# A hybrid decoder trunk: how the running-sum rows reach the SSD scan, and where its squares lie

## The chip, the cores and the metric

The kernel runs on one core of a Trainium2 chip. The metric is the device time of one execution in microseconds (us); the median of three runs counts. The kernel computes in float32.

## What is computed

Two layers and a final norm. The even layer projects the normed input once, and feeds a Mamba-2 SSD branch and a branch of differential attention; the odd layer is a gated linear recurrence. The change touches the SSD branch alone. Its scan, for 16 heads of 64 in 4 groups, sequence length 1024, chunks of 128:

```python
def ssd_scan(x, dt, A, Bm, Cm):
    ...
    a_cs = jnp.cumsum(a, axis=-1)
    CB = jnp.einsum("bclgn,bcsgn->bcgls", Cc, Bc)
    scores = CB[:, :, :, None] * jnp.exp(segsum(a))
    y_diag = jnp.einsum("bcgrls,bcsgrp->bclgrp", scores, X)
    decay_states = jnp.exp(a_cs[..., -1:] - a_cs)
    states = jnp.einsum("bclgn,bcgrl,bclgrp->bcgrpn", Bc, decay_states, X)
    ...
    y_off = jnp.einsum("bclgn,bcgrpn,bcgrl->bclgrp", Cc, prev, jnp.exp(a_cs))
    return (y_diag + y_off).reshape(b, L, H, P)
...
y = ssd_scan(xs, dt, A, Bm, Cm) + xs * D_skip[:, None]
y_a = rmsnorm(y * jax.nn.silu(z), ssd_norm_w)
```

So the running sum `a_cs` of a head enters twice: as exp of its differences inside a chunk (the scores), and as exp(a_cs) along the rows of the output (`y_off`). The norm at the end needs the sum of the squares of all the gated outputs.

## The kernel before

**Projections.** Activations lie with channels on partitions and time along the row, 1024 long. Each float32 operand is split into a high and a low part, and a product is three matmuls. A piece of a projection is 128 channels by 512 time steps: 24 matmuls of 128x512 (`mm_cm`, L174) into one of two PSUM buffers `pj`. Weights come by SyncE's queue into `w_raw` (L126); ScalarE casts the high part (L132) and VectorE makes the low one (L133). A conv piece is emptied from `pj` by ScalarE (L426, L427); after the fourth, VectorE does the other taps of the convolution (L435), ScalarE a tanh (L438), VectorE a product (L439). A gate piece is emptied by `silu2`: ScalarE's tanh from `pj` into the tile `th` (L232) and VectorE's product of `th` and `pj` into an `A` tile (L233). `pj` is free after L233.

**The scan.** The 32 chunk steps are 4 groups (of 4 heads) by 8 chunks. `weave` lets the steps of group g run between the pieces of the projection of group g+1 (12 pieces: 4 conv pieces of x, 4 of B and C, 4 of the gate z); the steps of the last group run between pieces of the attention's first head (q and k, v, gate). A step has two halves, `first(c)` and, two pieces later, `second(c)`.

- `first(c)` loads the running sum of the group's four heads for this chunk, the same for all 128 partitions (`R`, 128x4x128, L464), into one of three tiles that are used in turn: two called `G`, one `wT`. TensorE transposes x and B and multiplies B by C (L466 to L470) into PSUM tile `s1`; VectorE makes X (L475), GpSimd X times the decay (L478), ScalarE copies B (L479), VectorE masks CB (L480). VectorE subtracts the running sum of the partition's own time step from `R` (L482, four heads), ScalarE takes exp (L484), VectorE multiplies by CB (L485). X, the decayed X, the state and CB lie in one chunk tile `pk` (slots `p0`, `p0` and `bt` in turn).
- `second(c)` is the matmuls with the state, of the new state and of the scores (L502, L505, L508) into PSUM tile `big`; VectorE updates the state (L514, L515). For every second chunk it loads the running sum again for two chunks in another layout, two heads by 64 partitions each (L523, tile `ey`), and takes exp (L525). VectorE multiplies the state's part by it (L529) and adds the other part (L530). After an odd chunk it adds the D skip (L537, from the x tiles in `A`), multiplies by the gate (L540), ScalarE squares the result into a `th` tile (L542), GpSimd adds the squares up (L544, L547), and the result is stored (L548).

**Tiles.** A name in the trace is a slot: `t(tag)` waits until the tile that had the slot last has been read. There is one `th`, one `ey`, one `cm`, one `wT`, one `bt`, two `G`, two `p0`, two `o`, eleven `A`. `cm` is used by the first attention head afterwards, for its bias (loaded by L590, read by L607).

**Order.** In the scan TensorE's order is written out by hand (`manual_schedule`). The order of the other engines and of SyncE's queue is set by the framework's scheduler from the program's dependences.

Of the kernel before, what the change touches and what calls it, by code (L numbers as in the profile page):

```python
# [14 lines left out]
AF = mybir.ActivationFunctionType  # L15
# [4 lines left out]
P = 128  # L20
# [50 lines left out]
def run(pieces):  # L71
    for _ in pieces:
        pass
# [12 lines left out]
def bc(ap, shape):  # L86
    return ap.broadcast_to(shape)


class Net:  # L90
# [115 lines left out]
    def proj_v(self, u):  # L206
        vs = []
        run(self.v_pieces(u, vs))
        return self.v_of(vs)


    def gate_pieces(self, u, tags, gs):
# [240 lines left out]
def ssd_steps(S, g, tiles, ya, at, lag):  # L453


    nc = S.nc
    hs = slice(4 * g, 4 * g + 4)
    X_, sts, eas = {}, {}, {}

    def first(c):  # L460
        x0, x1, Bt, Ct = tiles[:4]
        cs = slice(c * P, c * P + P)
        R = S.t(("G", "G", "wT")[(8 * g + c) % 3], [P, 4, P])
        nc.sync.dma_start(R, bc(S.acs_d[hs, cs].unsqueeze(0), [P, 4, P]))  # L464
        pt = S.ps("s1")
        nc.tensor.matmul(pt[:, 384:512], lhsT=Bt[:, cs], rhs=Ct[:, cs], start=True, stop=True)  # L466
        for b in range(2):
            nc.tensor.transpose(out=pt[:, b * P:b * P + P], in_=(x0, x1)[b][:, cs], identity=S.ident)
        if c < NT - 1:
            nc.tensor.transpose(out=pt[:, 256:384], in_=Bt[:, cs], identity=S.ident)  # L470
        pk = S.t("bt" if (8 * g + c) % 3 == 2 else "p0", [P, 1024])
        X = pk[:, 0:256].rearrange("p (h d) -> p h d", d=64)
        Xd = pk[:, 256:512].rearrange("p (h d) -> p h d", d=64)
        cb, Bk = pk[:, 768:896], pk[:, 896:1024]
        nc.vector.tensor_tensor(X, pt[:, 0:256].rearrange("p (h d) -> p h d", d=64),  # L475
                                bc(S.dt[:, c, hs].unsqueeze(2), [P, 4, 64]), op=ALU.mult)
        if c < NT - 1:
            nc.gpsimd.tensor_tensor(Xd, X, bc(S.dec[:, c, hs].unsqueeze(2), [P, 4, 64]), op=ALU.mult)  # L478
            nc.scalar.copy(Bk, pt[:, 256:384])  # L479
        nc.vector.tensor_tensor(cb, pt[:, 384:512], S.triu, op=ALU.mult)  # L480
        for h in range(4):
            nc.vector.tensor_scalar(R[:, h], R[:, h], S.acs[:, c, 4 * g + h:4 * g + h + 1], 0.0,  # L482
                                    op0=ALU.subtract, op1=ALU.min)
        nc.scalar.activation(R, R, AF.Exp)  # L484
        nc.vector.tensor_tensor(R, R, bc(cb.unsqueeze(1), [P, 4, P]), op=ALU.mult)  # L485
        X_[c] = pk, R

    def second(c):
        Ct = tiles[3]
        cs = slice(c * P, c * P + P)  # L490
        pk, sc = X_[c]
        X = pk[:, 0:256].rearrange("p (h d) -> p h d", d=64)
        Xd = pk[:, 256:512].rearrange("p (h d) -> p h d", d=64)
        sn = pk[:, 512:768].rearrange("p (h d) -> p h d", d=64)
        Bk = pk[:, 896:1024]
        big = S.ps("big")
        pod = big[:, 0:512].rearrange("p (i b t) -> p i b t", i=2, b=2)
        pu = big[:, 512:768].rearrange("p (h d) -> p h d", d=64)
        st = sts.get(c - 1)
        if c > 0:  # L500
            for b in range(2):
                nc.tensor.matmul(pod[:, 0, b], lhsT=st[:, 2 * b:2 * b + 2, :], rhs=Ct[:, cs],  # L502
                                 start=True, stop=True)
        if c < NT - 1:
            nc.tensor.matmul(pu, lhsT=Bk, rhs=Xd, start=True, stop=True)  # L505
        for b in range(2):
            for hh in range(2):
                nc.tensor.matmul(pod[64 * hh:64 * hh + 64, 1, b], lhsT=X[:, 2 * b + hh],  # L508
                                 rhs=sc[:, 2 * b + hh], start=True, stop=True)
        if c < NT - 1:  # L510
            if c == 0:
                nc.scalar.copy(sn, pu)
            else:
                nc.vector.tensor_tensor(sn, st, bc(S.tot[:, c, hs].unsqueeze(2), [P, 4, 64]), op=ALU.mult)  # L514
                nc.vector.tensor_tensor(sn, sn, pu, op=ALU.add)  # L515
            sts[c] = sn
        xs, zg = tiles[:2], tiles[4]
        if c % 2 == 0:

            c2 = slice(c * P, (c + 2) * P)  # L520
            ea = S.t("ey", [P, 2, 256])
            for hh in range(2):
                nc.sync.dma_start(ea[64 * hh:64 * hh + 64],  # L523
                                  bc(S.acs_d[4 * g + hh:4 * g + 4:2, c2].unsqueeze(0), [64, 2, 256]))
            nc.scalar.activation(ea, ea, AF.Exp)  # L525
            eas[c // 2] = ea, S.t("o", [P, 2, 256])
        ea, tt = (z[:, :, (c % 2) * P:(c % 2) * P + P] for z in eas[c // 2])
        if c:
            nc.vector.tensor_tensor(tt, pod[:, 0], ea, op=ALU.mult)  # L529
            nc.vector.tensor_tensor(tt, tt, pod[:, 1], op=ALU.add)  # L530
        else:
            nc.vector.tensor_copy(tt, pod[:, 1])
        if c % 2 == 1:
            t = eas[c // 2][1]
            c2 = slice((c - 1) * P, (c + 1) * P)
            for b in range(2):
                nc.vector.scalar_tensor_tensor(t[:, b], xs[b][:, c2], S.dcol[:, 2 * g + b:2 * g + b + 1],  # L537
                                               t[:, b], op0=ALU.mult, op1=ALU.add)
            for b in range(2):
                nc.vector.tensor_tensor(t[:, b], t[:, b], zg[b][:, c2], op=ALU.mult)  # L540
            sq = S.t("th", [P, 2, 256])
            nc.scalar.activation(sq, t, AF.Square)  # L542
            if g == 0:
                nc.gpsimd.tensor_tensor(S.ysq[:, c2], sq[:, 0], sq[:, 1], op=ALU.add)  # L544
            else:
                for b in range(2):
                    nc.gpsimd.tensor_tensor(S.ysq[:, c2], S.ysq[:, c2], sq[:, b], op=ALU.add)  # L547
            S.ya_stored = nc.sync.dma_start(ya[2 * g:2 * g + 2, :, c2].rearrange("b p t -> p b t"), t)  # L548

    return [(at(c), 2 * c, lambda c=c: first(c)) for c in range(NT)] + [  # L550
        (at(c) + lag, 2 * c + 1, lambda c=c: second(c)) for c in range(NT)]


# [330 lines left out]
def layer0(S, x, x1_d, u1):  # L884
    nc, a = S.nc, S.a
# [4 lines left out]
    run(ssd_pieces(S, u, 0, tiles))  # L890
    with S.tc.issue_after(S.late):
        setup_rest(S)
    S.ysq = S.t("V", [P, L])
    with S.tc.manual_schedule(engines={mybir.EngineType.PE}):
        rest = []
# [266 lines left out]
@with_exitstack  # L1162
def trunk_kernel(ctx, tc, a, out):
    S = Net(ctx, tc, a)
    w0, w1 = wspecs(a)
    S.wspecs = w0 + w1
    x1_d = S.dram.tile([L, D], F32, name="x1_d")
    u1 = [None, None]
    layer0(S, a["x"][0], x1_d, u1)
    layer1(S, x1_d, u1, out)  # L1170
# [24 lines left out]
```

## Time and profile before

| | |
|---|---|
| median of 3 runs | 2238.65 us (2238.03 to 2240.89) |
| the profiled execution | 2242.69 us |
| its span | 2240.9 us |
| PE (TensorE, matmul) busy | 2178.8 us, 97% of the span |
| DVE (VectorE) | 1269.9 us, 57% |
| ACT (ScalarE) | 832.2 us, 37% |
| POOL (GpSimd) | 188.8 us, 8% |

Times in a row of the profile are in us unless marked ns. PE is TensorE's matmuls, PEld its weight loads, SP (or SPq) SyncE and its queue. A row of a timeline has the start, the length, the engine, the line, the operation, the tile written and those read with their shape, a count of instructions that stand together, and in brackets the engine's idle time before it and what ended it. PEclk is the clock that TensorE was granted, as a share of full speed.

### The profile page before, as it was taken

Reading aid. Unit: us, or ns where it says so; the run is one execution under the profiler, and the core shown is the slowest. Engines: PE = TensorE matmul, PEld = TensorE weight load, DVE = VectorE, ACT = ScalarE, POOL = GpSimd, SP = SyncE. Lnnn points to the kernel's source line nnn. Section 1 sums busy time; section 2 is a strip of 40 time slices with the busy share of each in tenths; the row PEclk is TensorE's granted clock in tenths of the full one; section 3 lists DMA queues with packets and bytes.
Section 4 is the critical chain, followed back from the end, with each engine's and each line's share of the span. In section 5 each row is a group of like instructions: output and inputs, shape, how many; then the busy total and the mean of one; then the engine's idle time right before and its main releaser. Section 6 shows DMA issues by size and latency. Waiting matters only on the chain.

```text
span 2240.9 us, 40897 instructions
## 1 busy us (share of the span) xinstructions
PE 2178.8 (97%) x16868; PEld 1920.3 (86%) x16868; DVE 1269.9 (57%) x2864; ACT 832.2 (37%) x1903; POOL 188.8 (8%) x216
## 2 busy tenths in 40 slices
PE   6998998899999999999999999999999999999998
PEld 5787776789898988999988989898989898989998
DVE  4765766565656556755453555555555555557444
ACT  4333333234444545644442323232323222324233
POOL 1001111110000000000010010101010101010000
PEclk9999999999999999999999999999999999999999
DMA  4322233332212221525331111111111111125333
GB/s 138 67 84 66 80 85 81 74 81 64 69 36 67 64 69 41 170 66 159 119 104 39 48 48 48 48 48 48 48 48 48 48 49 48 48 67 165 111 103 122
DMA packets 182256, 169.14 MB, mean 75 GB/s; under 512 B 10239, under 2 KB 163233, under 8 KB 182068
## 3 DMA queue, kind: packets, MB, share of 16 engines
q1 hardware_dynamic: 174564, 152.42, 23.1%
q0 software_dynamic: 3280, 9.90, 2.1%
q10 hardware_dynamic: 4224, 4.19, 0.6%
q8 instruction: 132, 2.16, 0.4%
q14 instruction: 56, 0.46, 0.1%
HBM read 132.66 MB, written 25.43 MB: 71 GB/s over the span
## 4 chain that ended last, share of the span: by engine, by line
PE 51%; DMA 1%; ACT 0%; DVE 0%; issue 0%; POOL 0%; POOLq 0%; ACTq 0%
PE pj L174 24%; PE pj L184 14%; PE big L184 5%; PE big L1051 2%; PE big L1139 1%; PE big L1141 1%; PE s L1128 1%; PE big L1093 1%; PE s L1155 1%; PE s L1122 1%; PE big L1087 0%; PE s L159 0%; DMA ey<-yb 0%; DMA th<-in_lvmask 0%; ACT w_hi L132 0%; DVE w_lo L133 0%
## 5 line engine op out<-in xcount | busy, mean ns | idle before, releaser
L174 PE MATMUL pj<-u,w_hi 128*128 128x512 f32 x3072 | 990.0, 400 | 31.3 <-DVE A L233 21.2
L174 PEld LDWEIGHTS pj<-u,w_hi 128*128 128x128 f32 x3072 | 573.4, 190 | 154.7 <-DVE A L233 23.0
L174 PE MATMUL pj<-u,w_lo 128*128 128x512 f32 x1536 | 607.9, 396 | 0.0
L184 PE MATMUL pj<-w_hi,u 128*128 128x256 f32 x2592 | 492.6, 286 | 1.0 <-DVE A L233 1.0
L184 PEld LDWEIGHTS pj<-w_hi,u 128*128 128x128 f32 x2592 | 409.9, 191 | 3.6 <-DVE A L233 1.4
L184 PE MATMUL pj<-w_lo,u 128*128 128x256 f32 x1296 | 368.3, 284 | 0.0
L174 PEld LDWEIGHTS pj<-u,w_lo 128*128 128x128 f32 x1536 | 291.8, 190 | 61.1 <-issue 0.2
L133 DVE TENSOR_TENSOR w_lo<-w_raw,w_hi 128x1024 fp32r<-128x1024 f32 x168 | 206.3, 1251 | 116.9 <-ACT w_hi L132 116.6
L184 PEld LDWEIGHTS pj<-w_lo,u 128*128 128x128 f32 x1296 | 247.8, 191 | 1.0
L132 ACT CAST w_hi<-w_raw 128x1024 fp32r<-128x1024 f32 x168 | 168.1, 1047 | 188.8 <-PE pj L174 107.6
L233 DVE SCALAR_TENSOR_TENSOR A<-th,pj 128x512 f32<-128x512 f32 x80 | 55.1, 689 | 140.9 <-ACT th L232 140.4
L232 ACT ACTIVATE th<-pj 128x512 f32<-128x512 f32 x96 | 57.2, 596 | 208.5 <-PE pj L174 190.8
L617 ACT ACTIVATE p<-p,mx 128x256 f32<-128x256 f32 (+7 forms) x128 | 98.5, 771 | 72.4 <-DVE mx L613 66.4
L148 POOL TENSOR_TENSOR ro<-rs_t,mhalf 128x4 f32<-128x4 f32 x48 | 52.8, 1100 | 682.4 <-DVE rs_t L147 489.1
L603 PE MATMUL big<-A 128*128 128x512 f32 (+3 forms) x384 | 90.3, 352 | 2.6 <-DMA A<-A 1.3
L968 POOL TENSOR_SCALAR A<-th,fN,fB 128x512 f32<-128x512 f32 x32 | 47.6, 1488 | 470.0 <-ACT th L965 470.0
L637 ACT COPY wT<-s 128x512 f32<-128x512 f32 (+2 forms) x96 | 45.8, 477 | 95.8 <-PE s L635 95.1
L639 PE MATMUL s<-V,wT 128*128 128x128 f32 x576 | 79.7, 275 | 0.6 <-ACT wT L637 0.6
L1035 DVE TENSOR_TENSOR A<-A,p 128x512 f32<-128x512 f32 x96 | 65.8, 686 | 23.5 <-PE big L1051 23.0
L639 PEld LDWEIGHTS s<-V,wT 128*128 128x128 f32 x576 | 74.4, 191 | 3.3 <-ACT wT L637 1.1
L1030 DVE TENSOR_TENSOR p<-p,p 128x512 f32<-128x512 f32 x96 | 66.2, 690 | 15.5 <-PE big L1087 6.2
L603 PEld LDWEIGHTS big<-A 128*128 128x128 f32 x384 | 64.5, 189 | 11.3 <-issue 2.3
(330 smaller groups left out, 2977.1 us busy)
## 6 DMA issues: line engine op xcount, KB each, us to landing
w_raw<-in_even_w_in SPq DMA_DIRECT2D x32, 512.0 KB, 4.7
w_raw<-in_odd_w_in SPq DMA_DIRECT2D x64, 256.0 KB, 3.3
w_raw<-in_odd_w_in SPq DMA_DIRECT2D x32, 512.0 KB, 3.9
w_raw<-in_even_w_in SPq DMA_DIRECT2D x48, 256.0 KB, 4.3
w_raw<-in_even_w_out SPq DMA_DIRECT2D x24, 512.0 KB, 4.4
w_raw<-in_odd_w_out SPq DMA_DIRECT2D x24, 512.0 KB, 4.6
A<-A POOLq DMA_DIRECT2D x32, 256.0 KB, 5.5
yo<-ey SPq DMA_DIRECT2D x32, 256.0 KB, 2.0
```

The source lines that it names most:

```text
L132: nc.scalar.copy(hq, raw)
L133: nc.vector.tensor_tensor(lq, raw, hq.bitcast(F32), op=ALU.subtract)
L148: return nc.gpsimd.tensor_tensor(dst, t[:, :n], self.mhalf[:, :n], op=ALU.pow)
L174: nc.tensor.matmul(out, lhsT=ww[:, k, ms], rhs=uu[k][:, sl], start=(n == 0), stop=(n == 3 * KT - 1))
L184: nc.tensor.matmul(out, lhsT=uu[k], rhs=ww[:, k, :], start=(k == 0 and j == 0), stop=(k == KT - 1 and j == 2))
L232: nc.scalar.activation(th, pj, AF.Tanh, scale=0.5)
L233: nc.vector.scalar_tensor_tensor(out, view(th), 1.0, view(pj), op0=ALU.add, op1=ALU.mult)
L603: nc.tensor.matmul(s[:, k0:k0 + kn], lhsT=q[:, isl], rhs=ks[j][:, k0:k0 + kn], start=(j == 0), stop=(j == 1))
L617: nc.scalar.activation(p[:, :n], p[:, :n], AF.Exp, bias=mx, accum_out=z)
L639: nc.tensor.matmul(po[:, i % 4, :], lhsT=wT[:, j * P:j * P + P], rhs=V(j, hh), start=(j == 0), stop=(j == i))
L1030: nc.vector.tensor_tensor(q, q, bc(t0, [P, L // (2 * h), h]), op=ALU.mult)
L1035: nc.vector.tensor_tensor(k, k, bc(halves(Ts[h], 1)[1], [P, L // (2 * h), h]), op=ALU.mult)
```

## The change

Three things are done together.

1. `rows_load(i)` loads the running sum of four heads for two chunks at once (128x4x256). The call stands in `first` of an even chunk and loads for the next pair; the first pair is loaded ahead of the scan. The pairs take the slots `G`, `G`, `wT` in turn. `first` uses its half of the tile.
2. The load in the other layout and its exp (L523, L525) are gone. `first` makes exp along the rows by two ScalarE instructions of 64 partitions by two heads by 128, read from the rows before L482 overwrites them, into `ey` or `cm` in turn, one tile for each chunk.
3. The squares of an odd chunk go into `pk[:, 0:512]`, where X and the decayed X of that chunk were, and not into `th`.

```diff
--- before.py
+++ after.py
@@ -207,6 +207,14 @@
         vs = []
         run(self.v_pieces(u, vs))
         return self.v_of(vs)
+
+
+    def rows_load(self, i):
+        if i < 16:
+            g, q = divmod(i, 4)
+            self.rows[i] = self.t(("G", "G", "wT")[i % 3], [P, 4, 256])
+            self.nc.sync.dma_start(self.rows[i], bc(
+                self.acs_d[4 * g:4 * g + 4, q * 256:q * 256 + 256].unsqueeze(0), [P, 4, 256]))
 
 
     def gate_pieces(self, u, tags, gs):
@@ -455,13 +463,15 @@
 
     nc = S.nc
     hs = slice(4 * g, 4 * g + 4)
-    X_, sts, eas = {}, {}, {}
+    X_, sts, ts = {}, {}, {}
 
     def first(c):
         x0, x1, Bt, Ct = tiles[:4]
         cs = slice(c * P, c * P + P)
-        R = S.t(("G", "G", "wT")[(8 * g + c) % 3], [P, 4, P])
-        nc.sync.dma_start(R, bc(S.acs_d[hs, cs].unsqueeze(0), [P, 4, P]))
+        if c % 2 == 0:
+
+            S.rows_load(4 * g + c // 2 + 1)
+        R = S.rows[4 * g + c // 2][:, :, (c % 2) * P:(c % 2) * P + P]
         pt = S.ps("s1")
         nc.tensor.matmul(pt[:, 384:512], lhsT=Bt[:, cs], rhs=Ct[:, cs], start=True, stop=True)
         for b in range(2):
@@ -478,17 +488,21 @@
             nc.gpsimd.tensor_tensor(Xd, X, bc(S.dec[:, c, hs].unsqueeze(2), [P, 4, 64]), op=ALU.mult)
             nc.scalar.copy(Bk, pt[:, 256:384])
         nc.vector.tensor_tensor(cb, pt[:, 384:512], S.triu, op=ALU.mult)
+
+        ea = S.t(("ey", "cm")[c % 2], [P, 2, P])
+        for hh in range(2):
+            nc.scalar.activation(ea[64 * hh:64 * hh + 64], R[64 * hh:64 * hh + 64, hh::2], AF.Exp)
         for h in range(4):
             nc.vector.tensor_scalar(R[:, h], R[:, h], S.acs[:, c, 4 * g + h:4 * g + h + 1], 0.0,
                                     op0=ALU.subtract, op1=ALU.min)
         nc.scalar.activation(R, R, AF.Exp)
         nc.vector.tensor_tensor(R, R, bc(cb.unsqueeze(1), [P, 4, P]), op=ALU.mult)
-        X_[c] = pk, R
+        X_[c] = pk, R, ea
 
     def second(c):
         Ct = tiles[3]
         cs = slice(c * P, c * P + P)
-        pk, sc = X_[c]
+        pk, sc, ea = X_[c]
         X = pk[:, 0:256].rearrange("p (h d) -> p h d", d=64)
         Xd = pk[:, 256:512].rearrange("p (h d) -> p h d", d=64)
         sn = pk[:, 512:768].rearrange("p (h d) -> p h d", d=64)
@@ -516,29 +530,22 @@
             sts[c] = sn
         xs, zg = tiles[:2], tiles[4]
         if c % 2 == 0:
-
-            c2 = slice(c * P, (c + 2) * P)
-            ea = S.t("ey", [P, 2, 256])
-            for hh in range(2):
-                nc.sync.dma_start(ea[64 * hh:64 * hh + 64],
-                                  bc(S.acs_d[4 * g + hh:4 * g + 4:2, c2].unsqueeze(0), [64, 2, 256]))
-            nc.scalar.activation(ea, ea, AF.Exp)
-            eas[c // 2] = ea, S.t("o", [P, 2, 256])
-        ea, tt = (z[:, :, (c % 2) * P:(c % 2) * P + P] for z in eas[c // 2])
+            ts[c // 2] = S.t("o", [P, 2, 256])
+        tt = ts[c // 2][:, :, (c % 2) * P:(c % 2) * P + P]
         if c:
             nc.vector.tensor_tensor(tt, pod[:, 0], ea, op=ALU.mult)
             nc.vector.tensor_tensor(tt, tt, pod[:, 1], op=ALU.add)
         else:
             nc.vector.tensor_copy(tt, pod[:, 1])
         if c % 2 == 1:
-            t = eas[c // 2][1]
+            t = ts[c // 2]
             c2 = slice((c - 1) * P, (c + 1) * P)
             for b in range(2):
                 nc.vector.scalar_tensor_tensor(t[:, b], xs[b][:, c2], S.dcol[:, 2 * g + b:2 * g + b + 1],
                                                t[:, b], op0=ALU.mult, op1=ALU.add)
             for b in range(2):
                 nc.vector.tensor_tensor(t[:, b], t[:, b], zg[b][:, c2], op=ALU.mult)
-            sq = S.t("th", [P, 2, 256])
+            sq = pk[:, 0:512].rearrange("p (b t) -> p b t", b=2)
             nc.scalar.activation(sq, t, AF.Square)
             if g == 0:
                 nc.gpsimd.tensor_tensor(S.ysq[:, c2], sq[:, 0], sq[:, 1], op=ALU.add)
@@ -890,6 +897,8 @@
     run(ssd_pieces(S, u, 0, tiles))
     with S.tc.issue_after(S.late):
         setup_rest(S)
+    S.rows = {}
+    S.rows_load(0)
     S.ysq = S.t("V", [P, L])
     with S.tc.manual_schedule(engines={mybir.EngineType.PE}):
         rest = []
```

What the scheduler makes of it, first at ScalarE, about 340 to 366 us in the trace of before: the tanh of a group's third gate piece. `L438` is the tanh of the convolution, `p_...` a chunk tile or the slot `p1`. Before:

```order
L438 ACTIVATE p_2606<-A 128x1024
L479 COPY bt<-s_2617 128x128
L484 ACTIVATE G<-G 128x512
L525 ACTIVATE ey<-ey 128x512
L479 COPY p_2702<-s_2697 128x128
L438 ACTIVATE p_2612<-A 128x1024
L542 ACTIVATE th<-o 128x512
L232 ACTIVATE th<-pj 128x512 x2
```

With the change:

```order
L446 ACTIVATE p_2599<-A 128x1024
L489 COPY bt<-s_2610 128x128
L494 ACTIVATE cm<-G 64x256 x2
L240 ACTIVATE th<-pj 128x512
L498 ACTIVATE G<-G 128x4x128
L489 COPY p_2695<-s_2690 128x128
L446 ACTIVATE p_2605<-A 128x1024
L240 ACTIVATE th<-pj 128x512
L549 ACTIVATE p_2515<-o 128x512
```

The first tanh of the two (L232, now L240) moved ahead of the squares and of the second `L438`; the two new exps (L494) stand ahead of it.

The same place on VectorE, up to the gate product L233. Before:

```order
L537 SCALAR_TENSOR_TENSOR o<-A,dcol,o 128x256 x2
L485 TENSOR_TENSOR wT<-wT,bt 128x512
L435 SCALAR_TENSOR_TENSOR A<-V,convw,A 128x1021
L480 TENSOR_TENSOR p_2702<-s_2697,triu 128x128
L540 TENSOR_TENSOR o<-o,A 128x256 x2
L485 TENSOR_TENSOR G<-G,p_2702 128x512
L439 SCALAR_TENSOR_TENSOR A<-p_2612,A 128x1024
L515 TENSOR_TENSOR bt<-bt,big 128x256
L529 TENSOR_TENSOR o<-big,ey 128x2x128
L514 TENSOR_TENSOR p_2702<-bt,ph 128x256
L530 TENSOR_TENSOR o<-o,big 128x2x128
L233 SCALAR_TENSOR_TENSOR A<-th,pj 128x512
```

With the change:

```order
L544 SCALAR_TENSOR_TENSOR o<-A,dcol,o 128x256 x2
L499 TENSOR_TENSOR G<-G,bt 128x4x128
L485 TENSOR_TENSOR p_2695<-s_2690,ph 128x256
L241 SCALAR_TENSOR_TENSOR A<-th,pj 128x512
L443 SCALAR_TENSOR_TENSOR A<-V,convw,A 128x1021
L547 TENSOR_TENSOR o<-o,A 128x256 x2
L490 TENSOR_TENSOR p_2695<-s_2690,triu 128x128
L499 TENSOR_TENSOR G<-G,p_2695 128x4x128
```

L233 (now L241) moved from behind the last product of the convolution and the next chunk's state to ahead of the last tap L435 (now L443).

VectorE again, at the last chunks of the scan, about 400 to 413 us: L570 (now L577) empties `pj` of the first q and k pieces, and needs an `A` tile that L537 (now L544) reads. Before:

```order
L529 TENSOR_TENSOR o<-big,ey 128x2x128
L570 SCALAR_TENSOR_TENSOR A<-pj,A 64x512
L530 TENSOR_TENSOR o<-o,big 128x2x128
L570 SCALAR_TENSOR_TENSOR A<-pj,A 64x512
L480 TENSOR_TENSOR p_2963<-s_2958,triu 128x128
L537 SCALAR_TENSOR_TENSOR o<-A,dcol,o 128x256 x2
L482 TENSOR_SCALAR wT<-wT,ph 128x128 x4
L485 TENSOR_TENSOR G<-G,p_2963 128x512
L540 TENSOR_TENSOR o<-o,A 128x256 x2
L570 SCALAR_TENSOR_TENSOR A<-pj,A 64x512 x2
```

With the change:

```order
L536 TENSOR_TENSOR o<-big,cm 128x2x128
L577 SCALAR_TENSOR_TENSOR A<-pj,A 64x512
L537 TENSOR_TENSOR o<-o,big 128x2x128
L577 SCALAR_TENSOR_TENSOR A<-pj,A 64x512
L490 TENSOR_TENSOR p_2954<-s_2949,triu 128x128
L496 TENSOR_SCALAR G<-G,ph 128x128 x3
L544 SCALAR_TENSOR_TENSOR o<-A,dcol,o 128x256 x2
L496 TENSOR_SCALAR G<-G,ph 128x128
L499 TENSOR_TENSOR G<-G,p_2954 128x4x128
L547 TENSOR_TENSOR o<-o,A 128x256 x2
L577 SCALAR_TENSOR_TENSOR A<-pj,A 64x512 x2
```

Three of the four L482 (now L496) moved ahead of L537; the two L570 of the later piece stay behind L540.

## Rows read from the trace of the kernel before

**Rows 1.** Busy time, 300:400: us, PE, PEld, DVE, ACT, POOL busy, PEclk, DMA, GB/s.

```profile
300.00:400.00 100.00, 89.86 (x468) 72.49 (x466) 65.76 (x135) 34.11 (x57) 14.16 (x16) 0.98 0.31 77
```

**Rows 2.** Waits in 85:490: engine, line, releaser, us in total, times, longest.

```profile
PE pj L174 <- DVE A L233: 21.2, 7, 5.6
```

**Rows 3.** Timeline of PE: the step after a gate piece, and three pauses.

```profile
352.66 0.38 PE L466 MATMUL s<-A 128*128 128x128 f32 x2
...
365.91 1.22 PE L174 MATMUL pj<-u,w_hi 128*128 128x512 f32 x2 [5.59 <-DVE A L233]
...
383.06 0.74 PE L174 MATMUL pj<-u,w_hi 128*128 128x512 f32 x2 [1.84 <-DVE A L233]
...
405.57 1.19 PE L174 MATMUL pj<-u,w_hi 128*128 128x512 f32 x2 [7.99 <-DVE A L570]
```

**Rows 4.** Busy time, the piece after each pause; columns as Rows 1.

```profile
289.39:296.58 7.19, 7.19 (x25) 5.75 (x25) 4.57 (x6) 2.40 (x4) 2.51 (x2) 0.76 0.62 182
365.91:372.94 7.03, 7.03 (x25) 5.67 (x25) 1.47 (x5) 1.23 (x2) 0.00 (x0) 0.78 0.10 13
383.06:388.68 5.62, 5.62 (x25) 4.62 (x25) 4.36 (x6) 2.41 (x4) 2.52 (x2) 1.00 0.55 152
405.57:413.17 7.60, 7.60 (x24) 6.11 (x25) 0.46 (x1) 0.00 (x0) 1.38 (x2) 0.71 0.10 35
sum 50.10, PE 50.09 PEld 40.28 DVE 18.55 ACT 10.90 POOL 7.31; mean PE 7.16 PEld 5.75 DVE 2.65 ACT 1.56 POOL 1.04
```

**Rows 5.** Timeline of DVE ahead of the long pause at 365.91.

```profile
353.31 0.87 DVE L482 TENSOR_SCALAR G<-G,ph 128x128 f32<-128x128 f32 x4 [1.12 <-DMA G<-acs_d]
...
359.05 1.27 DVE L435 SCALAR_TENSOR_TENSOR A<-V,convw,A 128x1021 f32<-128x1021 f32 x1
...
365.17 0.69 DVE L233 SCALAR_TENSOR_TENSOR A<-th,pj 128x512 f32<-128x512 f32 x1 [0.92 <-ACT th L232]
```

**Rows 6.** Timeline of ACT, the tanh of the same piece.

```profile
364.54 0.60 ACT L232 ACTIVATE th<-pj 128x512 f32<-128x512 f32 x1 [2.55 <-POOL V L547]
```

**Rows 7.** Timeline of DVE ahead of the short pause at 383.06.

```profile
380.07 0.29 DVE L482 TENSOR_SCALAR G<-G,ph 128x128 f32<-128x128 f32 x1 [3.22 <-DMA G<-acs_d]
...
382.32 0.68 DVE L233 SCALAR_TENSOR_TENSOR A<-th,pj 128x512 f32<-128x512 f32 x1
```

**Rows 8.** Groups on ACT in 90:480: busy us, mean ns, idle before.

```profile
L427 ACT ACTIVATE A<-pj,convb,convw 128x512 f32<-128x512 f32 x24 | 18.8, 783 | 3.4 <-DVE o L537 3.4
L426 ACT COPY V<-pj 128x512 f32<-128x512 f32 x24 | 13.8, 576 | 18.5 <-PE pj L174 18.5
L525 ACT ACTIVATE ey<-ey 128x512 f32<-128x512 f32 x16 | 10.1, 632 | 60.3 <-DMA ey<-acs_d 60.3
...
L512 ACT COPY p<-big 128x256 f32<-128x256 f32 x3 | 1.1, 358 | 0.0
```

**Rows 9.** Timeline of DVE ahead of the last pause at 405.57.

```profile
402.55 0.88 DVE L482 TENSOR_SCALAR wT<-wT,ph 128x128 f32<-128x128 f32 x4 [1.51 <-DMA wT<-acs_d]
```

**Rows 10.** Timeline of DVE: two L529, and the first reader of `cm`.

```profile
235.99 0.42 DVE L529 TENSOR_TENSOR o<-big,ey 128x256 f32<-128x256 f32 x1
...
475.50 0.42 DVE L529 TENSOR_TENSOR o<-big,ey 128x256 f32<-128x256 f32 x1 [0.58 <-PE big L508]
...
481.46 0.29 DVE L607 CUSTOM_DVE_ANT_0 p<-big,cm 128x128 f32<-128x128 f32 x1 [3.49 <-PE big L603]
```

**Rows 11.** Timeline of SP: eight loads of a head's bias.

```profile
472.92 4.72 SPq L590 DMA_DIRECT2D ph<-tz_d  x8
```

**Rows 12.** DMA issues in 118:480: count, KB each, median us to landing.

```profile
w_raw<-in_even_w_in SPq DMA_DIRECT2D x14, 512.0 KB, 5.0
...
G<-acs_d SPq DMA_DIRECT2D x20, 256.0 KB, 5.0
...
ph<-tz_d SPq DMA_DIRECT2D x16, 16.0 KB, 2.1
```

**Rows 13.** Timeline of PE: the last matmuls ahead of 235.99's L529.

```profile
231.08 0.66 PE L508 MATMUL big<-G,p 128*64 128x128 f32 x8
```

## The prediction

> **What bounds the kernel now.** I read the page's shares first, then the busy time by stretch, then what TensorE waits for, then the queues of VectorE and ScalarE just before those waits. Only the scan of the SSD half is touched, about 90 to 480 us of the span. TensorE is the engine that ends last there, but it isn't full: in the stretch shown it is busy 89.86 of 100 us, with VectorE at 65.76 and ScalarE at 34.11 [rows 1]. So no engine's total sets the pace; something arrives late.
>
> The waits view gives one cause for nearly all of it: the projection's matmuls (L174) wait for the gate product L233 seven times, 21.2 us together [rows 2]. The eighth large pause, 7.99 us at 405.57, waits for L570 [rows 3]. A projection piece is 24 matmuls into one of two `pj` buffers, so a piece can't begin until VectorE has emptied the buffer of the piece before last. Each group of heads but the last shows a long pause at its third gate piece (365.91, 5.59 us) and a short one at the piece after the next (383.06, 1.84 us) [rows 3].
>
> A pause costs more than its length. The page's clock by stretch is 1.00 for the piece after 383.06, which takes 5.62 us, and 0.78 after 365.91, where the piece takes 7.03; the seven pieces that follow the seven pauses over 1 us take 50.10 together [rows 4]. [...]
>
> **Why L233 is late.** At the long pause VectorE isn't idle but badly ordered: in the last 15 us before L233 at 365.17 it stands still for 1.12 us only (L482, rows of the running sum not yet landed) and 0.92 us (the tanh) [rows 5]. The tanh L232 had its input when TensorE went on to the scan's step at 352.66, but ran at 364.54: `th` is a single buffer, the squares L542 had been put into it, and GpSimd's sum L547 had to read them first [rows 3, 6]. At the short pause VectorE sat 3.22 us at L482 on a load of rows; L537, L540 and L233 stood behind it [rows 7].
>
> **The change, part by part.**
>
> *Squares leave `th`.* The tanh no longer waits for GpSimd. The order now has the tanh ahead of the second conv tanh on ScalarE, and L233 (there L241) ahead of the L435 that ran at 359.05. From the L515 before it up to that point VectorE runs the same twelve groups in both orders. They ended at 359.05 with the 1.12 us wait among them, so L233 would begin at 357.93 and end, at 0.69, at 358.6. TensorE wants the buffer at 365.91 - 5.59 = 360.32. The pause goes, with 1.7 us to spare [rows 3, 5]. What is late next is the L233 of the short pause, next paragraph.
>
> *Rows two chunks ahead, one load for two chunks.* In the new SyncE order each rows load stands at least one chunk pair before its use, so L482's waits for loads go. At the short pause L233 would start 3.22 us sooner, at 379.10, and end at 379.8; TensorE wants it at 383.06 - 1.84 = 381.22 [rows 3, 7]. Gone, with 1.4 us to spare. So all of the 21.2 us on L233 goes.
>
> *The added wait.* L482 overwrites rows that the new exp reads, so VectorE now waits for two ScalarE exps, and behind it stand L537, L540, L233. Nothing in this trace has 64 partitions by 256. The nearest row is the 128x256 copy at 0.36 us, the upper bound the 128x512 exp at 0.63, which is a larger tile and the same function [rows 8]; below, nothing is excluded down to none. I take 0.36, the row with the same length along a partition. Two of them, 0.72, fit into both margins (1.7 and 1.4); at 0.63 each, 1.26, they still do, barely. Cost taken: 0; if the cover is gone, 0.5 us at each of six places, 3 us in all.
>
> *ScalarE's total.* 64 exps by 0.36 is 23.0, less 16 of 0.632 (10.1), adds 12.9 us to an engine a third full [rows 1, 8]; hidden. [...] No trace here shows the 64-partition shape yet.
>
> *The clock.* Six of the seven slow pieces follow pauses that go; the seventh, at 405.57, took 7.60, so 1.98 of the 10.8 stays. Gain 8.8 [rows 4].
>
> *The last pause.* TensorE waits there for L570, that for L569, and that for a buffer of x which L537 of the last chunk must have read. L537 needs the scan's last matmuls, so this chain stays. Only the 1.51 us that L482 waited for a load, ahead of L570, goes [rows 9]; three of the four L482 now stand ahead of L537, which puts L569 off by 0.66 us but not L570, which is behind L540 in both orders. Gain 1.5, between 0 and all of it (7.99 + 1.98).
>
> *Removed loads.* 32 half-height loads of `ey` go, 4 MB; the 16 new loads carry what 32 did. ScalarE waited 60.3 us for `ey` [rows 8]; that is off the path except through what stood behind it.
>
> *What moves elsewhere.* `cm` now holds exps, so the first head's bias tile is loaded only after the last L529. That row is at 475.50 and the tile's first reader at 481.46 [rows 10]; eight such loads took 4.72 us to issue and land 2.1 us after [rows 11, 12]. Arrival at 475.9 + 6.8 = 482.7 would be 1.2 us late for VectorE, with a projection piece of 5.62 us on TensorE as cover: taken 0, bounds 0 and 1.2. At the start, the third of three 512 KB loads may come a landing late; loads of that size land in 5.0 us, and 256 KB of rows also in 5.0 [rows 12]. A gate's tanh stands behind its exp there: taken 0, bounds 0 and 5.0.
>
> **Sum.** 21.2 + 8.8 + 1.5 = 31.5 us. The profiled execution took 2242.69 with a span of 2240.9; that makes 2209.4 of span and 2211.2 of time. The median of the runs lies 4.04 below the profiled one, so against it: 2238.65 - 31.5 = 2207.2. Its own range: 2201 (most of the last pause goes too) to 2214 (3, 1.2 and half of 5.0 us come back).
>
> **Rivals.**
>
> *The short pauses stay*, because L482 waits for the exps instead of the load. For: the new wait stands at the same place. Against: it is at most 1.26 us where the load took 3.22. Three pauses of about 1.84 and the clock after two of them (7.19 against 5.62 [rows 4]) give back 5.5 + 3.1: 2215.8.
>
> *The long pauses stay*, because VectorE isn't ready sooner. For: it is busy nearly without a break before L233 [rows 5]. Against: the order now puts L233 before nine of the groups that it ran behind. The other 15.7 us of pauses and 5.6 of clock come back: 2228.5.
>
> *The rows aren't early after all*: SyncE's queue is in order and each rows load stands behind weight loads and stores that wait themselves. Then L482 waits as before, and the exps with it; nothing gained, 2238.7. Against: the buffers of rows come free more than two projection pieces before the load is needed.
>
> *Slower: ScalarE held by the exps.* An exp needs the buffer that L529 of two chunks earlier has read. Behind it on ScalarE stand the copies that empty `pj` (L426 0.58, L427 0.78 [rows 8]). L529 began as late as 4.25 us after its L508 ended (231.08 + 0.66 to 235.99 [rows 10, 13]). With two exps of 0.63 and the copies that is 6.87, 1.25 over a piece of 5.62. Over 32 chunks: 40 us, 2207 + 40 = 2247. It turns slower once a chunk loses more than 31.5 / 32 = 1.0 us. Against: that lateness came where VectorE had just stood waiting for rows.
>
> **How the numbers follow.** Forecast 0.67, short pauses stay 0.14, long ones stay 0.07, rows not early 0.04, slower 0.08. The range of 8 in 10 takes the forecast's own and the short pauses' case with the same costs on top (2215.8 + 3 + 1.2 + 2.5): 2201 to 2222. A measurement here tells about 0.2% (4.5 us) from no change; faster than that are the first three, 0.88; same 0.04; slower 0.08.
>
> **What would show it.** In the profile after: no wait of L174 for L233 over 1 us; no L482 waiting for a load after the first chunks; the tanh within 2 us of its gate piece; the clock at 1.00 except for one piece after the last pause, which shrinks to about 6.5 us. Wrong would be: TensorE waiting for L427 or for the product L485, ScalarE's new exps over 0.63 us or waiting long for L529, or a pause at the scan's start.

## The result, and the profile after

| | before | after |
|---|---|---|
| median of the runs | 2239.77 us (2238.03 to 2243.48, 4 runs) | 2212.26 us (2210.89 to 2213.12, 4 runs) |
| profiled execution, its span | 2242.69, 2240.9 us | 2210.89, 2209.1 us |

The ratio is 0.9874 with a 95% interval of 0.9857 to 0.9892: 27.5 us faster, between 24.2 and 32.0. The forecast was 2207.2, in a range of 2201 to 2222.

The changed kernel's page, span and shares: TensorE's busy time fell by 10 us while its work is the same, ScalarE's rose by 19.

```profile
span 2209.1 us, 40847 instructions
...
PE 2168.9 (98%) x16868; PEld 1914.3 (87%) x16868; DVE 1267.0 (57%) x2864; ACT 851.6 (39%) x1951; POOL 190.1 (9%) x216
```

What TensorE waits for in 85:450, the scan (line, releaser, us in total, times, longest us). Against [rows 2]: the gate product, L241 now, has three waits of 0.56 us left where L233 had seven of 21.2 together. L577 is the L570 of before.

```profile
PE pj L174 <- DVE A L577: 6.4, 1, 6.4
PE pj L174 <- DVE A L241: 1.7, 3, 0.6
PE pj L174 <- ACT A L435: 0.6, 2, 0.3
```

TensorE's timeline, the places that answer to [rows 3] (start, us, ... idle before and releaser); 351.63 is the step that stood ahead of the short pause:

```profile
351.63 0.38 PE L476 MATMUL s<-A 128*128 128x128 f32 x2
...
352.79 0.73 PE L174 MATMUL pj<-u,w_hi 128*128 128x512 f32 x2 [0.56 <-DVE A L241]
...
373.66 1.19 PE L174 MATMUL pj<-u,w_hi 128*128 128x512 f32 x2 [6.39 <-DVE A L577]
```

Busy time by stretch for the piece behind each of those two (columns of [rows 1]); against [rows 4], only the piece behind the last pause is still slow, at a granted clock of 0.74:

```profile
352.79:358.37 5.58, 5.58 (x24) 4.62 (x25) 3.95 (x6) 1.30 (x2) 0.00 (x0) 1.00 0.46 115
373.66:381.03 7.37, 7.37 (x24) 5.93 (x25) 0.46 (x1) 0.00 (x0) 1.39 (x2) 0.74 0.10 36
```

**Where the time went.** TensorE's order in the scan is the same in both kernels, so the start of each chunk step (its first matmul, L466 before, L476 after) can be set side by side. The lead of the changed kernel grows in steps, and each step is one pause:

| chunk step | start before | start after | lead | gained there | the pause of before |
|---|---|---|---|---|---|
| 5 | 165.72 | 163.41 | 2.31 | | 0.69 at 101.90 |
| 6 | 184.66 | 176.60 | 8.06 | 5.75 | 4.09, long |
| 8 | 209.18 | 198.17 | 11.01 | 2.95 | 1.91, short |
| 14 | 279.29 | 260.26 | 19.03 | 8.02 | 5.23, long |
| 16 | 303.73 | 281.84 | 21.89 | 2.86 | 1.82, short |
| 22 | 372.94 | 343.95 | 28.99 | 7.10 | 5.59, long |
| 24 | 395.83 | 365.52 | 30.31 | 1.32 | 1.84, short |
| 25 | 413.17 | 381.03 | 32.14 | 1.83 | 7.99, the last |

What a step gains over its pause is mostly the clock: the first long pause of 4.09 also had a piece of 7.19 us behind it, at a granted clock of 0.76, where 5.62 is the undisturbed one, 5.66 together; behind the second, of 5.23, the piece took 8.29 at 0.65. Of the first 2.31 us, 0.69 are a pause on L233; the other 1.62 lie ahead of the scan, 0.95 of them ahead of TensorE's first matmul (11.11 us before, 10.16 after), which the change doesn't touch. From the scan's end on the lead stays, 31.8 us of span.

Single executions differ by such amounts outside the scan. In the twelve traces of this record (before, after and the ten below) the first chunk step starts between 115.3 and 118.5 us, and from the start of the last one to the end of the span it takes between 1777.3 (e6) and 1781.4 (after), though the code behind the scan is the same. So a difference of a few us between two kernels is one of the scan only if its steps or pauses show it.

### The profile page after: what moved, and what is told of

It is laid out like the page before. It is cut to its first block, busy times and chain, and to the rows that moved or that the text cites. A ratio compares the mean times of both kernels' runs of the same rounds, so it can differ in the third digit from the quotient of the medians.

```text
span 2209.1 us, 40847 instructions
## 1 busy us (share of the span) xinstructions
PE 2168.9 (98%) x16868; PEld 1914.3 (87%) x16868; DVE 1267.0 (57%) x2864; ACT 851.6 (39%) x1951; POOL 190.1 (9%) x216
## 4 chain that ended last, share of the span: by engine, by line
PE 52%; DMA 1%; ACT 0%; DVE 0%; issue 0%; POOL 0%; POOLq 0%; ACTq 0%
PE pj L174 24%; PE pj L184 14%; PE big L184 5%; PE big L1060 2%; PE big L1148 1%; PE big L1150 1%; PE s L1137 1%; PE big L1102 1%; PE s L1164 1%; PE s L1131 1%; PE big L1096 0%; DMA ey<-yb 0%; PE s L159 0%; DMA th<-in_lvmask 0%; ACT w_hi L132 0%; DVE w_lo L133 0%
## 5 line engine op out<-in xcount | busy, mean ns | idle before, releaser
L133 DVE TENSOR_TENSOR w_lo<-w_raw,w_hi 128x1024 fp32r<-128x1024 f32 x168 | 204.7, 1242 | 118.5 <-ACT w_hi L132 118.3
L241 DVE SCALAR_TENSOR_TENSOR A<-th,pj 128x512 f32<-128x512 f32 x80 | 55.1, 689 | 141.7 <-ACT th L240 135.3
L240 ACT ACTIVATE th<-pj 128x512 f32<-128x512 f32 x96 | 57.2, 596 | 194.2 <-PE pj L174 193.9
L443 DVE SCALAR_TENSOR_TENSOR A<-V,convw,A 128x1023 f32<-128x1023 f32 (+2 forms) x48 | 61.5, 1285 | 22.9 <-ACT A L435 22.8
```

What stands on the lines that cost most here:

```text
L133: nc.vector.tensor_tensor(lq, raw, hq.bitcast(F32), op=ALU.subtract)
L240: nc.scalar.activation(th, pj, AF.Tanh, scale=0.5)
L241: nc.vector.scalar_tensor_tensor(out, view(th), 1.0, view(pj), op0=ALU.add, op1=ALU.mult)
L443: nc.vector.scalar_tensor_tensor(cv[:, d:], rp[:, :L - d], S.convw[:, k, ci:ci + 1], cv[:, d:], op0=ALU.mult, op1=ALU.add)
```

## The experiments

Ten kernels, each beside runs of the kernel before on the same chip, whose median was 2239.98 us beside e1 to e4, 2239.05 beside e5 to e8 and 2241.05 beside e9 and e10:

| run | what it is | median us | TensorE's waits in the scan: gate product; q/k product |
|---|---|---|---|
| e1 | before, squares moved alone | 2217.24 | 1.57, 1.59, 1.43; 8.10 |
| e2 | after, squares back in `th` | 2223.92 | 2.15, 3.15, 3.15 and 3 x 0.56; 6.39 |
| e3 | after, the old exp along rows | 2218.07 | 2.44, 1.76, 1.98; 8.58 |
| e4 | after, a gate tile in `V` | 2201.34 | 2 x 0.56; 1.54 |
| e5 | after, removed loads added again | 2212.28 | 0.38, 3 x 0.56; 6.39 |
| e6 | after, three tiles for the exps | 2212.95 | 0.92, 1.12, 1.80; 6.39 |
| e7 | after, exps twice | 2209.32 | 3 x 0.56; 6.39 |
| e8 | after, rows for one chunk | 2211.13 | 3 x 0.56; 7.54 |
| e9 | e4, steps 1.3 pieces apart | 2198.17 | none |
| e10 | e4, 1.3 in the third group alone | 2200.94 | 2 x 0.56; none |

### Which part does what: e1 and e2

```diff
-            sq = S.t("th", [P, 2, 256])
+            sq = pk[:, 0:512].rearrange("p (b t) -> p b t", b=2)
```

> The kernel before with only the squares moved into the chunk's own tile; rows and the loads of ey as before. Theory (the tanh of the gate waits for th, the rows' load makes the short pauses): the three long pauses (4.09, 5.23 and 5.59 us) go with the clock lost behind them, together about 21 us as the changed kernel's landmarks show (5.75, 8.00 and 7.09 there); the short ones (1.91, 1.82, 1.84) and the last (7.99) stay. 2240 - 21 = 2219, between 2216 and 2223. Rival (the late rows make the long pauses too): they stay at over 3 us each, 2232 or more.

Measured 2217.24 (ratio 0.9901, 0.9885 to 0.9916). The chunk steps behind the three long pauses gain 5.75, 8.00 and 7.10 us, the same as with the whole change: moving the squares out of `th` is enough to end the long pauses. The short ones stay, at 1.43 to 1.59. But the clock behind them is back, which was not expected. The three pieces behind the short pauses in e1, by stretch:

```profile
187.95:193.57 5.62, 5.62 (x25) 4.66 (x26) 3.67 (x6) 3.83 (x6) 0.74 (x1) 1.00 0.27 70
273.55:279.17 5.62, 5.62 (x25) 4.66 (x26) 4.56 (x6) 2.73 (x4) 1.48 (x2) 1.00 0.36 108
358.10:363.72 5.62, 5.62 (x25) 4.66 (x26) 3.32 (x5) 4.05 (x6) 1.48 (x2) 1.00 0.14 48
```

The other way round, the changed kernel with the squares in `th`:

```diff
-            sq = pk[:, 0:512].rearrange("p (b t) -> p b t", b=2)
+            sq = S.t("th", [P, 2, 256])
```

> The changed kernel with the squares back in th: rows for two chunks early, exps along the rows on ScalarE, nothing else. Theory: L240 still waits until GpSimd has read the squares, so the long pauses stay at some 3 to 5 us each (all of VectorE's work is about 1 us earlier, no more); the short ones shrink to 0.6 as in the changed kernel, the last to 6.4. Saved: 3 x 1.3, 3 of clock, 1.8, and 3 x 1 of the long ones: 12, so 2228, between 2223 and 2233. Rival (early rows alone do it): 2213.

Measured 2223.92 (0.9919 to 0.9946): the theory, at the low end. ScalarE's and then GpSimd's timeline ahead of the third long pause of e2 show the mechanism in three rows: the squares L549 go into `th`, GpSimd reads them for 2.72 us, and the tanh L240 starts when it is done.

```profile
345.92 0.61 ACT L549 ACTIVATE th<-o 128x512 f32<-128x512 f32 x1
...
349.36 0.60 ACT L240 ACTIVATE th<-pj 128x512 f32<-128x512 f32 x1 [2.83 <-POOL V L554]
```

```profile
346.61 2.72 POOL L554 TENSOR_TENSOR V<-V,th 128x256 f32<-128x256 f32 x2 [0.54 <-ACT th L549]
```

The long pauses are shorter than before, 2.15, 3.15 and 3.15 us, since VectorE reaches the products L547 sooner, which the squares read; the pieces behind them take 7.08, 7.17 and 7.17 us, at a granted clock of 0.76, 0.76 and 0.75 over 173.87:180.50, 262.26:269.50 and 350.73:357.50. The gains of the two halves, 22.7 and 16.1 us, come to more than the whole, since both shorten the long pauses and each takes away clock losses that the other also takes: e1 those behind the short pauses (1.00 there, where two of the three had 0.76 before), too.

### What removed the short pauses: e3, e5, e6 and e8

e3 keeps the early rows and the moved squares, and has the old loads into `ey` with their exp of 128x512:

```diff
-        ea = S.t(("ey", "cm")[c % 2], [P, 2, P])
-        for hh in range(2):
-            nc.scalar.activation(ea[64 * hh:64 * hh + 64], R[64 * hh:64 * hh + 64, hh::2], AF.Exp)
...
+            ea = S.t("ey", [P, 2, 256])
+            for hh in range(2):
+                nc.sync.dma_start(ea[64 * hh:64 * hh + 64],
+                                  bc(S.acs_d[4 * g + hh:4 * g + 4:2, c2].unsqueeze(0), [64, 2, 256]))
+            nc.scalar.activation(ea, ea, AF.Exp)
...
```

> The changed kernel with the old way to exp along the rows (loads of the second layout into ey for two chunks, one exp of 128x512), rows early and squares in the chunk tile kept. Theory: neither the 64 small exps nor the 4 MB of loads that they replace are on the path: 2212, between 2210 and 2215. Rival (the loads of ey held the multiply with them on VectorE, and with it the gate product): the short pauses come back at 1.8 us, with clock, 2218 to 2222.

Measured 2218.07 (0.9892 to 0.9920): the theory fell, and the rival's time came. Its cause, though, isn't the rival's. VectorE in e3 ahead of the short pause of the last group (L492 is the subtraction, L496 in the changed kernel):

```profile
356.92 1.07 DVE L492 TENSOR_SCALAR G<-G,ph 128x128 f32<-128x128 f32 x5 [2.42 <-DMA G<-acs_d]
...
358.83 0.68 DVE L241 SCALAR_TENSOR_TENSOR A<-th,pj 128x512 f32<-128x512 f32 x1
```

SyncE issued that load of rows at 351.51, 5.4 us earlier:

```profile
351.51 0.37 SPq L216 DMA_DIRECT2D G<-acs_d  x1
```

So VectorE waits for rows after all, and the gate product stands behind the wait. In the changed kernel the load comes no earlier: it is issued at 346.21, 5.42 us ahead of the step at 351.63; in e3 the lead of that step is 23.64 and not 28.99, so the same moment would be 351.56. Nor does it come earlier than in the kernel before: the load of the rows that made the short pause there ([rows 7]) was issued at 375.16, and 375.16 less the lead of 28.99 is 346.17. SyncE of the kernel before:

```profile
375.16 0.36 SPq L464 DMA_DIRECT2D G<-acs_d  x1
```

The difference is the order. SyncE, ScalarE and VectorE of the changed kernel at that load:

```profile
346.21 0.37 SPq L216 DMA_DIRECT2D G<-acs_d  x1
```

```profile
360.83 1.75 ACT L494 ACTIVATE ey<-G 64x256 f32<-64x256 f32 x4 [6.74 <-DVE o L536]
```

```profile
349.37 0.76 DVE L547 TENSOR_TENSOR o<-o,A 128x256 f32<-128x256 f32 x2
352.05 0.69 DVE L241 SCALAR_TENSOR_TENSOR A<-th,pj 128x512 f32<-128x512 f32 x1 [1.93 <-PE s L476]
...
361.29 1.81 DVE L496 TENSOR_SCALAR G<-G,ph 128x128 f32<-128x128 f32 x8
```

The eight L496 of the next pair stand behind L241, because they must follow the exps, and the exps wait 6.74 us for L536 of two chunks earlier to free their tile. Two kernels were to tell whether this order is the cause. e5 leaves it and brings the loads back:

```diff
-            ts[c // 2] = S.t("o", [P, 2, 256])
+            c2 = slice(c * P, (c + 2) * P)
+            e2 = ts[c // 2] = S.t("o", [P, 2, 256])
+            for hh in range(2):
+                nc.sync.dma_start(e2[64 * hh:64 * hh + 64],
+                                  bc(S.acs_d[4 * g + hh:4 * g + 4:2, c2].unsqueeze(0), [64, 2, 256]))
+            nc.scalar.activation(e2, e2, AF.Exp)
```

> The changed kernel, and the removed loads and exps of the second layout put back beside the new ones (into the tile o, in which the output is made afterwards; their values aren't used). VectorE's order is that of the changed kernel: L496 of the next pair stays behind the gate product L241. Theory (the short pauses depend on whether L496, which waits for rows, stands ahead of L241): 2212, between 2210 and 2215, TensorE's pauses 0.56 as there. Rival (the loads of the second layout cost time by themselves, on SyncE's queue or the DMA engines): 2217 or more, pauses near 2 us as where they were kept.

Measured 2212.28, the changed kernel's own time, with its pauses: 32 loads of 4 MB in all and 16 exps cost nothing there. The rival of e3 is out. e6 changes the order and leaves the loads alone:

```diff
...
-        ea = S.t(("ey", "cm")[c % 2], [P, 2, P])
+        ea = S.t(("ey", "cm", "junk")[(8 * g + c) % 3], [P, 2, P], mybir.dt.bfloat16)
```

> The changed kernel, but the exps along the rows go to three tiles in turn, not two, each in bfloat16 so that they fit (ey, cm, junk). An exp no longer waits for L536 of two chunks earlier, and the scheduler puts the eight L496 of the next pair ahead of the gate product L241. Theory (order decides): VectorE waits there for rows that land some 5 us after their slot came free, about 2.4 us; the short pauses are back at 1.7 to 2.5 us, with some clock: 2216 to 2221. Rival (the rows come early enough wherever L496 stands): 2211 to 2213, and more room for the exps does no harm.

Measured 2212.95 (2210.02 to 2214.37): in time this is no change, as the rival had it, but the trace has the theory's mechanism at half its size. ScalarE waits 3.62 us for the rows, VectorE 2.38 for ScalarE, and L241 stands behind; ScalarE and then VectorE of e6:

```profile
352.81 0.85 ACT L494 ACTIVATE ey<-G 64x256 bf16<-64x256 f32 x2 [3.62 <-DMA G<-acs_d]
```

```profile
353.25 0.28 DVE L496 TENSOR_SCALAR G<-G,ph 128x128 f32<-128x128 f32 x1 [2.38 <-ACT ey L494]
...
354.38 0.68 DVE L241 SCALAR_TENSOR_TENSOR A<-th,pj 128x512 f32<-128x512 f32 x1
```

The three pauses are 0.92, 1.12 and 1.80 instead of 0.56, 2.2 us more in all, and the pieces behind them take 5.62, 5.58 and at most 5.63 us (from the end of L241 at 355.06 to the next step at 360.69), as an undisturbed one does; the medians can't tell 2.2 us. In e3 the same three are 2.44, 1.76 and 1.98, and the last pause is 2.19 longer: 6.7 us. Behind the 2.44 the piece takes 7.17 us, 1.5 us more; together that is the 8.2 us by which e3's scan is longer than the changed kernel's in the traces (319.82 against 311.63 from the first chunk step to the last), where the medians differ by 5.8. So the order is a cause that two traces show; that it is all of e3's loss is worked out from its pauses, not shown by a run that mends them.

In e8 the rows come for one chunk at a time, one chunk ahead:

```diff
...
-            self.rows[i] = self.t(("G", "G", "wT")[i % 3], [P, 4, 256])
+            self.rows[i] = self.t(("G", "G", "wT")[i % 3], [P, 4, P])
...
-        if c % 2 == 0:
-            S.rows_load(4 * g + c // 2 + 1)
+        S.rows_load(8 * g + c + 1)
...
```

> The changed kernel, but the rows are loaded for one chunk at a time (256 KB, 32 loads) and one chunk ahead. Theory (a load lands about 5 us after its slot comes free, and a slot comes free over two projection pieces, 11 us, before its use): 2211 to 2215. Rival (two chunks at once and two ahead are needed): the short pauses come back, 2217 to 2222.

Measured 2211.13 (2209.12 to 2211.43): theory. Two chunks in one load, and two ahead, aren't needed. The last pause is 7.54 here and not 6.39, as VectorE's order is another there; the time doesn't show it.

### Whether the exps press ScalarE: e7

```diff
         for hh in range(2):
-            nc.scalar.activation(ea[64 * hh:64 * hh + 64], R[64 * hh:64 * hh + 64, hh::2], AF.Exp)
+            for _ in range(2):
+                nc.scalar.activation(ea[64 * hh:64 * hh + 64], R[64 * hh:64 * hh + 64, hh::2], AF.Exp)
```

> The changed kernel with each of the 64 exps along the rows made twice. At 0.416 us each that is 27 us more of ScalarE's time, 0.83 a chunk. Theory (ScalarE has room, the exps are off the path): 2212 to 2216. Rival (the exps and the copies that empty pj already fill a projection piece on ScalarE): nearly all of it shows, 2230 or more, with TensorE waiting for L435.

Measured 2209.32 (2209.05 to 2210.14). One of the four groups of exps in e7 (busy us, mean ns, idle before):

```profile
L495 ACT ACTIVATE cm<-G 64x256 f32<-64x256 f32 x44 | 18.3, 416 | 7.8 <-DVE o L537 6.8
```

27 us more of ScalarE's work cost nothing, and TensorE's pauses are those of the changed kernel. The rival of a full ScalarE is refuted. That the median is below the 2212 expected, and 2.9 us lower than the changed kernel's, comes with no shorter scan (311.60 us from the first chunk step to the last, against 311.63); of the two traces this one is 1.9 us shorter behind the scan, inside the spread there, and more isn't known.

### What is left: e4, e9 and e10

By the traces the 0.56 us and the last pause are one thing, a wait for an `A` slot. L241 at 352.05 waits for L476 at 351.63, which reads B of the group before for the last time. And the L576 that empty `pj` at the last pause, ScalarE of the changed kernel:

```profile
366.71 1.07 ACT L576 ACTIVATE A<-pj 64x512 fp32r<-64x512 f32 x2 [2.89 <-PE big L516]
...
370.96 1.08 ACT L576 ACTIVATE A<-pj 64x512 fp32r<-64x512 f32 x2 [2.27 <-DVE o L544]
```

The second q tile can only have the slot of x that L544 reads. e4 puts the last group's second gate tile into a `V` slot that is free by then:

```diff
-    for _ in S.gate_pieces(u, "AA", zg):
+    for _ in S.gate_pieces(u, "AV" if g == 3 else "AA", zg):
```

> The changed kernel, and the second gate tile of the last group goes to a V slot, so one A slot more is free from there on. Theory (TensorE's last pause and the 0.56 us pauses are waits for an A slot: q's second tile can only have the slot of x that L544 of the last chunk reads): the pause of 6.39 falls to about 0.8, the clock behind it (7.37 for a piece against 5.62) comes back, one of the 0.56 goes: 5.6 + 1.75 + 0.6 = 8 us, 2204, between 2202 and 2207. Rival (L577 is late because it stands behind L499 and L547 on VectorE, not for the slot): 2 us at most, 2210 to 2212.

Measured 2201.34 (2201.05 to 2202.79), ratio 0.9832: 10.9 us less than the changed kernel, where 8 were expected. The 0.56 of the last group is gone and the other two stay, as worked out, and the four L576 no longer wait for L544; ScalarE of e4:

```profile
358.95 0.59 ACT L576 ACTIVATE A<-pj 64x512 fp32r<-64x512 f32 x1 [3.64 <-PE pj L174]
...
366.10 0.59 ACT L576 ACTIVATE A<-pj 64x512 fp32r<-64x512 f32 x1 [1.89 <-PE pj L174]
367.10 0.59 ACT L576 ACTIVATE A<-pj 64x512 fp32r<-64x512 f32 x1 [0.40 <-PE big L516]
```

The last pause is 1.54 and the piece behind it takes 5.62 at a clock of 1.00, by stretch:

```profile
369.19:374.81 5.62, 5.62 (x25) 4.67 (x26) 4.13 (x12) 1.55 (x3) 0.63 (x1) 1.00 0.38 111
```

By the starts of the chunk steps the scan gains 7.5 us, as worked out; some 3 more are gained between 850 and 1040 us, in the last heads of the attention and the output projection, where single waits come out shorter. The traces of the other kernels differ there by as much, so this part isn't settled and is not put down to the slot.

The slots come free earlier if the last chunk's steps come earlier. On top of the edit of e4:

```diff
-                steps = ssd_steps(S, g, tiles, ya, lambda c: 1.5 + 1.5 * c, 2)
+                steps = ssd_steps(S, g, tiles, ya, lambda c: 1.5 + 1.3 * c, 2)
```

> The kernel with the second gate tile of the last group in a V slot, and the chunk steps of the first three groups set 1.3 pieces apart, not 1.5, so that the last chunk's steps come a piece earlier and the A tiles of a group come free earlier. Theory (the pauses left are waits for an A slot): 0.56 twice and 1.54 go, 2.7 us: 2198.6, between 2197 and 2201. Rival (VectorE can't keep up with steps at 1.3 pieces while it does the taps of the convolution): pauses of other lines appear, 2202 or more.

Measured 2198.17 (2196.75 to 2199.70), ratio 0.9814 (0.9801 to 0.9828). TensorE has no wait left in the scan, by stretch in e9:

```profile
85.00:450.00 365.00, 365.00 (x1994) 300.40 (x1993) 250.82 (x548) 153.71 (x278) 56.38 (x66) 1.00 0.32 81
```

> The same with 1.3 pieces in the third group alone. Theory: only the 1.54 goes and one A slot comes free a piece earlier at the start of the attention's projection: 2199.8, between 2198 and 2202; with the rival of the run before it lies between that run and 2201.3, or above both.

Here 1.3 holds for the third group alone (`(1.3 if g == 2 else 1.5) * c`). Measured 2200.94 (2199.39 to 2202.27): the 1.54 is gone, the two 0.56 stand, as expected, but against e4 the time can't tell it. e9 beats both kernels, by 14 us and 43 us.

## Why the prediction was right, and where its steps failed

The forecast of the likeliest case came: faster, inside the range, with the long and the short pauses gone but for 1.7 us. Of its two causes the squares are shown as it had them; the early rows work in another way than it said. By the prediction's own steps:

- **Squares leave `th`: right.** e1 takes the long pauses away by this alone. L241 was put at 357.93 in the time of before; less the lead of 21.90 that is 336.03, and it ran at 334.50. VectorE and ScalarE there, after the change:

```profile
334.50 0.67 DVE L241 SCALAR_TENSOR_TENSOR A<-th,pj 128x512 f32<-128x512 f32 x1
335.09 1.27 DVE L443 SCALAR_TENSOR_TENSOR A<-V,convw,A 128x1021 f32<-128x1021 f32 x1
```

```profile
330.96 0.60 ACT L240 ACTIVATE th<-pj 128x512 f32<-128x512 f32 x1 [2.39 <-PE pj L174]
```

  The tanh now waits for its piece of projection and for nothing else.
- **"All of the 21.2 us on L233 goes": mis-sized by 1.7.** 1.68 us stay, three waits of 0.56. The step put L233 at 379.10 since VectorE would be free; the tile that it writes wasn't. Its `A` slot is held until the chunk step that ran at 380.62 in the time of before. What is late next was looked for among VectorE's instructions, not among the slots of the output.
- **"L482's waits for loads go", because rows are loaded early: right in effect, wrong in its reason.** The rows, issued at 346.21 and landing 5.6 us later by the median of such loads, are there 9 us ahead of their use at 360.83 only because the order puts the use later. This load comes no earlier than the one of the kernel before (375.16 less the lead). Where L492 or L496 stands ahead of the gate product (e3, e6), VectorE waits for the same load again. The added wait, which the prediction took as a cost to be covered, is what puts L496 behind; that this helped was luck, as no step of the prediction had it.
- **The exps: right that they are hidden, the price was low.** 0.36 was taken, 0.416 measured, inside the bounds; the 64 exps less the 16 of before add 16.5 us to ScalarE and not 12.9:

```profile
L494 ACT ACTIVATE ey<-G 64x256 f32<-64x256 f32 x22 | 9.2, 417 | 19.5 <-DVE o L536 15.1 <-DMA G<-acs_d 4.1
```

  e7 shows that even twice the price is hidden. One of the prediction's signs of being wrong did come, exps that wait long for the multiply (L529, now L536): 6.74 us at 360.83, and 15.1 in all in the group above. TensorE lost nothing by it.
- **The clock: 8.8 forecast, 9.0 measured** (before, seven pieces took 50.10 us, 10.76 more than seven undisturbed ones of 5.62, the prediction's 10.8; after, one took 1.75 more).
- **The last pause: 1.5 forecast, 1.60 measured** (7.99 to 6.39).
- **Removed loads, the first head's bias, the scan's start: 0 forecast.** e5 confirms the first; TensorE has no wait for the others.
- **From the profiled execution to the median: the step that failed.** The terms come to 19.5 + 9.0 + 1.6 = 30.1 us where 31.5 were forecast. Against the profiled execution the forecast was 2211.2, and 2210.89 came; that it is this close is luck, as the 1.62 us ahead of the scan, which no term has, make up for the 1.4 missing. For the median the prediction took the whole 31.5 from 2238.65, as if the 4.04 us by which the profiled execution lay above it were all outside of what the change removes. By the medians 27.5 came, 4.0 less; with 1.1 by which the median of all runs of before lies above that of the first three, 2207.2 is 5.1 us too low. The profiled execution of before lay 2.9 us above the median of the runs now known, the changed kernel's 1.4 below its own. Where the other executions differ isn't shown, since one of each kernel was traced.

Of the rivals, "short pauses stay" is seen in e6, with VectorE waiting for the exps as it said, at half the size. "The rows aren't early after all" had its premise right at the load of 346.21; with the order of the changed kernel that costs nothing, and in e3, with another order, the short pauses come back by it. "The long pauses stay" comes in e2, but for `th` and not because VectorE isn't ready. "ScalarE held by the exps" fell with e7.

## What to carry to other kernels

When an engine waits for a product to empty PSUM, list everything that the product itself needs: its input's buffer, the instructions ahead of it in its queue, and the slot that it writes. A load is early only against the place where the order puts its reader, so after adding a dependence look where the scheduler put the instructions on both sides of it. A forecast made on one profiled execution should say how far that execution lies from the median, and should not take for granted that the median falls by the whole sum.

## What the runs showed of the hardware

- A pause of TensorE doesn't always cost clock, and its length alone doesn't tell. In the kernel before, the pieces behind pauses of 1.91 and 1.82 us ran at a granted clock of 0.76 in the mean and took 7.18 and 7.19 us (by stretches of 1 us it fell to 0.50 and was at 1.00 again from 198.85 and from 294.39 on); the one behind 1.84 ran at 1.00 and took 5.62. All three came 17 to 18 us after a long pause. In e1, without the long pauses, those behind 1.57, 1.59 and 1.43 ran at 1.00, and so did the one behind 1.54 in e4; behind 1.76 and 1.98 in e3 the pieces took 5.58 and 5.60 us, behind 1.80 in e6 at most 5.63. In e2 a pause of 2.15 was followed by a piece of 7.08, and in e3 one of 2.44 by one of 7.17.
- An exp of 64x256, a quarter of the tile, takes 0.416 us where one of 128x512 takes 0.63 ([rows 8]), whether 64 or 128 of them run (after, e7).
- 4 MB of loads more in the scan did not move the time: 2212.28 us in e5 against 2212.26 in the changed kernel, where 0.30 of the DMA engines' time was in use over 85:450.
